# Two chained matrix products with a GELU between: an opening block that goes slice by slice, and fp32r operands in six of sixteen contraction tiles

## The chip, the cores and the metric

The kernel runs on one core of one Trainium2 chip. The core has several engines that run side by side and wait for each other through semaphores: PE (TensorE, matrix products; its weight loads are listed apart as PEld), DVE (VectorE), ACT (ScalarE), POOL (GpSimd) and SP (SyncE, which here only issues transfers). Sixteen DMA engines move data between HBM and the on-chip memory SBUF; PE writes its sums to a second on-chip memory, PSUM. The metric is the device time of one execution in microseconds (us); lower is better.

## The reference

```python
def setup_inputs():
    m, k, n, p = 1024, 1024, 2048, 1024      # a: m x k, b: k x n, c: n x p, all float32, normal
...
def reference(a, b, c):
    h = np.matmul(a, b)
    h = 0.5 * h * (1 + np.tanh(np.sqrt(2 / np.pi) * (h + 0.044715 * h ** 3)))
    return np.matmul(h, c).astype(np.float32)
```

The inputs are 4.19 MB (a), 8.39 MB (b) and 8.39 MB (c), the output is 4.19 MB. Each of the two products has 1024 x 1024 x 2048 multiplications. On PE that is 256 matmuls each, if one matmul takes a 128 x 128 stationary operand (the weights) and streams 512 columns past it.

## The kernel before, in words

All inputs are float32 in HBM; they are loaded into staging buffers, cast to bf16 and kept in SBUF. The rows of a are worked through in two chunks of 512 (mc = 0 and 1).

For each chunk `load_a_chunk` (L47) loads four row tiles of 128 x 1024, each by one transfer on the SP queue (L51), casts each on ACT (L53), and transposes it on PE in 32 pieces of 128 x 128 (L60, out to the PSUM tile `pt`), which DVE copies one by one into the eight tiles `aT` (L61). So `aT` is a chunk of a with the contraction index on the partitions.

Then comes the first product. Its result is made transposed, with n on the partitions: for each of 16 column tiles `nt` of b, eight matmuls over the contraction tiles `kt` are accumulated in one PSUM tile of 128 x 512 (L90); b is the stationary operand, `aT` is streamed. ACT applies the GELU on the way out of PSUM and writes the bf16 tile `hT` (L93). In chunk 0 b is loaded in four column slices of 512: `load_b_slice` (L65) issues eight transfers on SP (L68), and ACT casts each piece (L69). Before each column tile of chunk 0 `load_c` (L71) loads one 128 x 1024 tile of c on POOL's queue (L73), which DVE casts (L74). In chunk 1 b and c are there already.

The second product of the chunk follows (L96 to L105): for each of four row tiles and two halves of the columns, 16 matmuls over `nt` are accumulated (L100), with `hT` stationary and `c_sb` streamed; DVE copies the sum to SBUF (L104) and SP stores it (L105).

The order on each engine is settled by the tile framework's scheduler from the order of the program and from the dependences; the buffer counts of the pools (six staging buffers for a and b, three for c, three PSUM tiles for sums, two for transposes) decide how far a transfer or a product can run ahead. Transfers of one queue start in the order of their issue.

Of the kernel before, what the change touches and what calls it, by code (L numbers as in the profile page):

```python
# [1 line left out]

# [6 lines left out]

F32 = mybir.dt.float32  # L10
BF16 = mybir.dt.bfloat16
AF = mybir.ActivationFunctionType


@with_exitstack
def kernel(ctx, tc, a, b, c, out):
    nc = tc.nc
    M, K = a.shape
    _, N = b.shape
    _, P = c.shape  # L20
    KT = K // 128
    NT = N // 128
    MC = 512
    PC = 512
    BS = 512
    NSL = N // BS

    consts = ctx.enter_context(tc.tile_pool(name="consts", bufs=1))
    ident = consts.tile([128, 128], BF16)
    make_identity(nc, ident)  # L30

    bpool = ctx.enter_context(tc.tile_pool(name="bpool", bufs=KT))
    cpool = ctx.enter_context(tc.tile_pool(name="cpool", bufs=NT))
    stage = ctx.enter_context(tc.tile_pool(name="stage", bufs=6))
    cstage = ctx.enter_context(tc.tile_pool(name="cstage", bufs=3))

    abfpool = ctx.enter_context(tc.tile_pool(name="abfpool", bufs=5))
    atpool = ctx.enter_context(tc.tile_pool(name="atpool", bufs=KT + 2))
    hpool = ctx.enter_context(tc.tile_pool(name="hpool", bufs=NT + 2))
    psum = ctx.enter_context(tc.tile_pool(name="psum", bufs=3, space=bass.MemoryType.PSUM))  # L40
    psum_t = ctx.enter_context(tc.tile_pool(name="psum_t", bufs=2, space=bass.MemoryType.PSUM))
    opool = ctx.enter_context(tc.tile_pool(name="opool", bufs=4))

    b_sb = [bpool.tile([128, N], BF16, name="b_sb") for _ in range(KT)]
    c_sb = [cpool.tile([128, P], BF16, name="c_sb") for _ in range(NT)]

    def load_a_chunk(mc):  # L47
        a_bf = []
        for mt in range(MC // 128):
            st = stage.tile([128, K], F32, name="sta")  # L50
            nc.sync.dma_start(out=st, in_=a[ds(mc * MC + mt * 128, 128), :])  # L51
            t = abfpool.tile([128, K], BF16, name="a_bf")
            nc.scalar.activation(t, st, AF.Copy)  # L53
            a_bf.append(t)
        aT = []
        for kt in range(KT):
            at = atpool.tile([128, MC], BF16, name="aT")
            for mt in range(MC // 128):
                pt = psum_t.tile([128, 128], BF16, name="pt")
                nc.tensor.transpose(pt, a_bf[mt][:, ts(kt, 128)], ident)  # L60
                nc.vector.tensor_copy(at[:, ts(mt, 128)], pt)  # L61
            aT.append(at)
        return aT

    def load_b_slice(j):  # L65
        for kt in range(KT):
            st = stage.tile([128, BS], F32, name="stb")
            nc.sync.dma_start(out=st, in_=b[ts(kt, 128), ts(j, BS)])  # L68
            nc.scalar.activation(b_sb[kt][:, ts(j, BS)], st, AF.Copy)  # L69

    def load_c(nt):  # L71
        st = cstage.tile([128, P], F32, name="stc")
        nc.gpsimd.dma_start(out=st, in_=c[ts(nt, 128), :])  # L73
        nc.vector.tensor_copy(c_sb[nt], st)  # L74

    aT = load_a_chunk(0)
    hT_all = []
    for mc in range(M // MC):
        if mc > 0:
            aT = load_a_chunk(mc)  # L80
        hT = []
        for j in range(NSL):
            if mc == 0:
                load_b_slice(j)
            for nt in range(j * (NT // NSL), (j + 1) * (NT // NSL)):
                if mc == 0:
                    load_c(nt)
                ps = psum.tile([128, MC], F32, name="ps1")
                for kt in range(KT):
                    nc.tensor.matmul(ps, b_sb[kt][:, ts(nt, 128)], aT[kt],  # L90
                                     start=(kt == 0), stop=(kt == KT - 1))
                h = hpool.tile([128, MC], BF16, name="hT")
                nc.scalar.activation(h, ps, AF.Gelu_apprx_tanh)  # L93
                hT.append(h)

        for mt in range(MC // 128):  # L96
            for pc in range(P // PC):
                ps = psum.tile([128, PC], F32, name="ps2")
                for nt in range(NT):
                    nc.tensor.matmul(ps, hT[nt][:, ts(mt, 128)],  # L100
                                     c_sb[nt][:, ts(pc, PC)],
                                     start=(nt == 0), stop=(nt == NT - 1))
                ot = opool.tile([128, PC], F32, name="ot")
                nc.vector.tensor_copy(ot, ps)  # L104
                nc.sync.dma_start(out=out[ds(mc * MC + mt * 128, 128), ts(pc, PC)], in_=ot)  # L105


# [1 line left out]
_INS = ['a', 'b', 'c']  # L109
_OUTS = [((1024, 1024), 'float32')]  # L110


# [23 lines left out]
```

## Time and profile before

| what | value |
|---|---|
| time, median of the two runs shown | 195.03 us (157.47 and 232.58) |
| span of the profiled execution | 157.0 us (time of the run that it answers to: 157.47 us) |
| mean granted TensorE clock | 0.946 |
| PE busy | 125.8 us, 80% of the span |
| ACT, DVE, POOL busy | 47.6, 33.7, 9.3 us |
| read from HBM, written | 20.97 MB, 4.19 MB |
| transfers: time from issue to landing, median | a 7.9 us, b 7.5 us, c 6.8 us, output 2.0 us |

The profile is of one execution on the chip. A group line of the page reads: line of the kernel, engine, operation, what it writes and reads, shapes and types, how many, then busy time in us and mean ns of one, then the idle time of the engine just before these instructions and what ended it. In the strip of 40 slices each digit is the busy share of a slice of the span in tenths; PEclk is the granted clock of TensorE in tenths. Matmuls overlap in PE's pipeline, so the mean duration of one (from its start to its end) is longer than the distance between two starts. Some matmul records are missing from the trace, so the counts of matmuls are slightly below those of the code.

### The profile page before, as it was taken

How to read it: one execution, taken by the hardware profiler on the slowest of the kernel's cores; microseconds unless marked ns; L12 is line 12 of the kernel's file. 1: busy time of each engine (PE TensorE's matmuls, PEld its weight loads, DVE VectorE, ACT ScalarE, POOL GpSimd, SP SyncE). 2: the span in 40 equal slices, each digit the busy share in tenths (PEclk: the TensorE clock that was granted, in tenths of full speed). 3: DMA queues.
4: the chain of work that ended last, by engine and by line, in shares of the span. 5: the costliest groups of instructions: out<-in, count | busy, mean ns of one | idle time of the engine just before them, and what ended most of it. 6: DMA issues, size and time to landing. Idle time of an engine off the chain costs nothing.

```text
span 157.0 us, 1522 instructions
## 1 busy us (share of the span) xinstructions
PE 125.8 (80%) x565; PEld 56.4 (36%) x576; DVE 33.7 (21%) x96; ACT 47.6 (30%) x74; POOL 9.3 (6%) x22
## 2 busy tenths in 40 slices
PE   0104952729994699999999979999999999999990
PEld 0001421213441244444444434444444444444440
DVE  0022664423113100011122146600000002111111
ACT  3534734497563995300000000053343310000000
POOL 6010121221210000000000000000000000000000
PEclk9999997555999789999999999999999999999999
DMA  5999999999999930011111120000000001122111
GB/s 177 406 381 316 362 338 413 397 399 401 395 399 398 410 155 2 0 67 71 67 67 69 69 103 30 0 4 0 0 0 0 0 4 67 67 84 112 72 67 67
DMA packets 10375, 25.26 MB, mean 161 GB/s; under 512 B 1152, under 2 KB 1152, under 8 KB 10368
## 3 DMA queue, kind: packets, MB, share of 16 engines
q1 hardware_dynamic: 8064, 16.78, 29.0%
q0 software_dynamic: 2304, 8.39, 13.6%
q8 instruction: 4, 0.07, 0.2%
q14 instruction: 3, 0.02, 0.1%
HBM read 20.97 MB, written 4.19 MB: 160 GB/s over the span
## 4 chain that ended last, share of the span: by engine, by line
PE 62%; DMA 26%; ACT 5%; DVE 2%; SPq 2%; issue 1%
PE ps L100 35%; DMA stb<-in_b_dram 26%; PE ps L90 24%; ACT b_sb L69 3%; PE pt L60 2%; ACT hT L93 2%; SPq L51 1%; DVE aT L61 1%; DVE ot L104 1%; ACT L93 1%; SPq L68 1%
## 5 line engine op out<-in xcount | busy, mean ns | idle before, releaser
L90 PE MATMUL ps<-aT,b_sb 128*128 128x512 bf16 x250 | 66.8, 410 | 8.9 <-ACT hT L93 7.1
L100 PE MATMUL ps<-c_sb,hT 128*128 128x512 bf16 x251 | 55.3, 379 | 0.3
L90 PEld LDWEIGHTS <-b_sb 128*128 128x128 bf16 x256 | 26.2, 103 | 48.7 <-issue 20.3
L100 PEld LDWEIGHTS <-hT 128*128 128x128 bf16 x256 | 25.0, 98 | 30.2
L93 ACT ACTIVATE hT<-ps 128x512 bf16<-128x512 f32 x32 | 18.6, 594 | 56.7 <-PE ps L90 55.6
L104 DVE COPY ot<-ps 128x512 f32<-128x512 f32 x16 | 11.1, 692 | 81.8 <-PE ps L100 81.8
L60 PE MATMUL pt<-ident,a_bf 128*128 128x128 bf16 x64 | 13.3, 240 | 18.4 <-ACT a_bf L53 11.7
L69 ACT ACTIVATE b_sb<-stb 128x512 bf16<-128x512 f32 x32 | 19.8, 629 | 15.1 <-DMA stb<-in_b_dram 14.8
L74 DVE CAST c_sb<-stc 128x1024 bf16<-128x1024 f32 x16 | 11.1, 692 | 27.2 <-DMA stc<-in_c_dram 27.1
L61 DVE COPY aT<-pt 128x128 bf16<-128x128 bf16 x64 | 12.5, 220 | 11.4 <-PE pt L60 10.8
L60 PEld LDWEIGHTS <-a_bf 128*128 128x128 bf16 x64 | 6.7, 107 | 17.7 <-ACT a_bf L53 12.3
L73 POOL DMA_DIRECT2D stc<-in_c_dram x16 | 8.6, 539 | 35.1 <-DVE aT L61 23.0
L53 ACT ACTIVATE a_bf<-sta 128x1024 bf16<-128x1024 f32 x8 | 8.4, 1054 | 6.3 <-DMA sta<-in_a_dram 6.3
L53 ACT ACT_TABLE_LOAD x1 | 1.3, 1283 | 0.7 <-PEq L120 0.7
L93 ACT ACT_TABLE_LOAD x1 | 1.3, 1283 | 0.0
masks.py:199 POOL TENSOR_SCALAR_AFFINE_SELECT ident<-ident 128x128 bf16<-128x128 bf16 x1 | 0.3, 306 | 0.1
masks.py:197 POOL MEMSET ident<- 128x128 bf16 x1 | 0.2, 205 | 0.3 <-POOLq L120 0.3
L120 POOL MEMSET const-float32-0.0<- 128x1 f32 x1 | 0.1, 99 | 0.2 <-issue 0.2
L120 POOL MEMSET const-bfloat16-1.0<- 128x1 bf16 x1 | 0.1, 102 | 0.0
L120 POOL MEMSET const-uint8-127<- 128x1 uint8 x1 | 0.1, 102 | 0.0
L120 POOL MEMSET const-float32-1.0<- 128x1 f32 x1 | 0.1, 99 | 0.0
## 6 DMA issues: line engine op xcount, KB each, us to landing
stc<-in_c_dram POOLq DMA_DIRECT2D x16, 512.0 KB, 6.8
stb<-in_b_dram SPq DMA_DIRECT2D x32, 256.0 KB, 7.5
sta<-in_a_dram SPq DMA_DIRECT2D x8, 512.0 KB, 7.9
out_dram<-ot SPq DMA_DIRECT2D x16, 256.0 KB, 2.0
```

The lines of the kernel that those rows point to most:

```text
L51: nc.sync.dma_start(out=st, in_=a[ds(mc * MC + mt * 128, 128), :])
L53: nc.scalar.activation(t, st, AF.Copy)
L60: nc.tensor.transpose(pt, a_bf[mt][:, ts(kt, 128)], ident)
L61: nc.vector.tensor_copy(at[:, ts(mt, 128)], pt)
L68: nc.sync.dma_start(out=st, in_=b[ts(kt, 128), ts(j, BS)])
L69: nc.scalar.activation(b_sb[kt][:, ts(j, BS)], st, AF.Copy)
L73: nc.gpsimd.dma_start(out=st, in_=c[ts(nt, 128), :])
L74: nc.vector.tensor_copy(c_sb[nt], st)
L90: nc.tensor.matmul(ps, b_sb[kt][:, ts(nt, 128)], aT[kt], start=(kt == 0), stop=(kt == KT - 1))
L93: nc.scalar.activation(h, ps, AF.Gelu_apprx_tanh)
L100: nc.tensor.matmul(ps, hT[nt][:, ts(mt, 128)], c_sb[nt][:, ts(pc, PC)], start=(nt == 0), stop=(nt == NT - 1))
L104: nc.vector.tensor_copy(ot, ps)
```

## The change

The order on the engines is now that of the program, by a manual schedule. The kernel holds all of a transposed (`aT[k][h]`, two halves of 512 rows), b as one tile, and all of `hT`, and there is no longer a loop over row chunks.

- **Opening block.** a is loaded in eight slices along the contraction index (all 1024 rows x 128 columns, so rows of 512 bytes in HBM), each followed by the matching 128 rows of the first three column tiles of b. For each slice DVE casts two halves of a, ACT casts b, PE makes eight transposes into two PSUM tiles of 128 x 512, and DVE copies one of them and ACT the other into `aT`. The six sums of the first three column tiles (three tiles x two halves of rows) lie open in six PSUM tiles at once, and each slice adds six matmuls to them. The second half of a slice is done after the transposes of the next one. Ahead of it stand seven matmuls on zeros (they add to nothing that is kept) and one GELU of a single column.
- **Loads.** All loads go on the SP queue, but for the first piece of b, which ACT issues; DVE casts the rest of b and c, in transfers of 0.5 to 1 MB. POOL issues none.
- **First product, rest.** For each of the other 13 column tiles, two groups of eight matmuls, each followed by its GELU.
- **Second product.** 16 contraction tiles as before, for eight row tiles. The first six of them (R = 6) have `hT` and c in fp32r, a four-byte format that PE takes as an operand, written by ACT and DVE; the other ten stay bf16. For the last row tile the second half of the columns is made and stored in two parts of 256.

```diff
-    consts = ctx.enter_context(tc.tile_pool(name="consts", bufs=1))
...
+    ctx.enter_context(tc.manual_schedule())
+    astage = ctx.enter_context(tc.tile_pool(name="astage", bufs=4))
+    abf = ctx.enter_context(tc.tile_pool(name="abf", bufs=3))
+    b0stage = ctx.enter_context(tc.tile_pool(name="b0stage", bufs=4))
+    stage = ctx.enter_context(tc.tile_pool(name="stage", bufs=4))
+    ppool = ctx.enter_context(tc.tile_pool(name="ppool", bufs=6, space=PSUM))
+    tpool = ctx.enter_context(tc.tile_pool(name="tpool", bufs=2, space=PSUM))
...
+    R = 6
+    F32R = mybir.dt.float32r
+    c_r = keep.tile([128, R, P], F32R, name="c_r")
+    c_h = keep.tile([128, NT - R, P], BF16, name="c_h")
+    hT = [[keep.tile([128, H], F32R if t < R else BF16, name=f"hT{t}_{h}") for h in range(2)] for t in range(NT)]
...
+    for k in range(KT):
+        st = astage.tile([128, MT, 128], F32, name="a_st")
+        bt = b0stage.tile([128, W0], F32, name="b0_st")
+        if k == 0:
+            nc.sync.dma_start(out=st[:, 0:4, :], in_=av[:, 0:4, ts(k, 128)])
+            nc.scalar.dma_start(out=bt, in_=bv[:, k, 0:W0])
+            nc.sync.dma_start(out=st[:, 4:8, :], in_=av[:, 4:8, ts(k, 128)])
+        else:
+            nc.sync.dma_start(out=st, in_=av[:, :, ts(k, 128)])
+            nc.sync.dma_start(out=bt, in_=bv[:, k, 0:W0])
...
+    nc.scalar.activation(g, warm[:, 0:1], AF.Gelu_apprx_tanh)
+    for _ in range(7):
+        nc.tensor.matmul(wps, warm[:, 0:128], warm, start=True, stop=True)
...
+    def mm0(k, h):
+        for t in range(N0):
+            nc.tensor.matmul(ps[t][h], b_sb[:, k, ts(t, 128)], aT[k][h],
+                             start=(k == 0), stop=(k == KT - 1))
+    for k in range(KT):
+        ab = abf.tile([128, MT, 128], BF16, name="ab")
+        nc.vector.tensor_copy(ab[:, 0:4, :], a_st[k][:, 0:4, :])
+        nc.vector.tensor_copy(ab[:, 4:8, :], a_st[k][:, 4:8, :])
+        nc.scalar.activation(b_sb[:, k, 0:W0], b_st[k], AF.Copy)
+        for h in range(2):
+            pt = tpool.tile([128, H], BF16, name="pt")
+            for j in range(4):
+                nc.tensor.transpose(pt[:, ts(j, 128)], ab[:, 4 * h + j, :], ident)
+            if h == 0:
+                nc.vector.tensor_copy(aT[k][h], pt)
+            else:
+                nc.scalar.activation(aT[k][h], pt, AF.Copy)
+        if k > 0:
+            mm0(k - 1, 1)
+        mm0(k, 0)
+    mm0(KT - 1, 1)
+    def load_b(t0, nt):
+        w = nt * 128
+        kn = 2048 // max(w, 256)
+        for kh in range(0, KT, kn):
+            st = stage.tile([128, 2048], F32, name="st")
+            sv = st[:, 0:kn * w].rearrange("p (k n) -> p k n", k=kn)
+            nc.sync.dma_start(out=sv, in_=bv[:, kh:kh + kn, ds(t0 * 128, w)])
+            nc.vector.tensor_copy(b_sb[:, kh:kh + kn, ds(t0 * 128, w)], sv)
+    def load_c(t0):
+        st = stage.tile([128, 2048], F32, name="st")
+        sv = st.rearrange("p (t q) -> p t q", t=2)
+        nc.sync.dma_start(out=sv, in_=cv[:, t0:t0 + 2, :])
+        nc.vector.tensor_copy(c_r[:, t0:t0 + 2, :] if t0 < R else c_h[:, t0 - R:t0 - R + 2, :], sv)
...
+    def mm1(t):
+        for h in range(2):
+            p = ppool.tile([128, H], F32, name="ps")
+            for k in range(KT):
+                nc.tensor.matmul(p, b_sb[:, k, ts(t, 128)], aT[k][h],
+                                 start=(k == 0), stop=(k == KT - 1))
+            nc.scalar.activation(hT[t][h], p, AF.Gelu_apprx_tanh)
...
+    for mt in range(MT):
+        h, j = divmod(mt, 4)
+        for q0, w in ((0, 512), (512, 512)) if mt < MT - 1 else ((0, 512), (512, 256), (768, 256)):
+            p = ppool.tile([128, w], F32, name="ps", padded_shape=[128, H])
+            for t in range(NT):
+                nc.tensor.matmul(p, hT[t][h][:, ts(j, 128)], c_r[:, t, ds(q0, w)] if t < R else c_h[:, t - R, ds(q0, w)],
+                                 start=(t == 0), stop=(t == NT - 1))
+            store(mt, q0, w, p)
```

More of the change, by code (lines that the diff above doesn't have):

```diff
@@ L12 @@
 AF = mybir.ActivationFunctionType
+PSUM = bass.MemoryType.PSUM
 @with_exitstack
@@ L22 @@
     NT = N // 128
[L23 to L26, printed above, removed]
-    consts = ctx.enter_context(tc.tile_pool(name="consts", bufs=1))
-    ident = consts.tile([128, 128], BF16)
-    make_identity(nc, ident)
[L32 to L105, printed above, removed]
@@ new lines @@
+    b0stage = ctx.enter_context(tc.tile_pool(name="b0stage", bufs=4))
+    stage = ctx.enter_context(tc.tile_pool(name="stage", bufs=4))
+    opool = ctx.enter_context(tc.tile_pool(name="opool", bufs=4))
+    ppool = ctx.enter_context(tc.tile_pool(name="ppool", bufs=6, space=PSUM))
+    tpool = ctx.enter_context(tc.tile_pool(name="tpool", bufs=2, space=PSUM))
+    warm = consts.tile([128, H], BF16, name="warm")
+    nc.vector.memset(warm, 0.0)
+    ident = consts.tile([128, 128], BF16, name="ident")
@@ new lines @@
+    make_identity(nc, ident)
+    aT = [[keep.tile([128, H], BF16, name=f"aT{k}_{h}") for h in range(2)] for k in range(KT)]
+    b_sb = keep.tile([128, KT, N], BF16, name="b_sb")
+    R = 6
[3 more added lines that the diff above has]
+    hT = [[keep.tile([128, H], F32R if t < R else BF16, name=f"hT{t}_{h}") for h in range(2)] for t in range(NT)]
+    a_st, b_st = [], []
+    for k in range(KT):
[8 more added lines that the diff above has]
+            nc.sync.dma_start(out=bt, in_=bv[:, k, 0:W0])
+        a_st.append(st)
+        b_st.append(bt)
@@ new lines @@
+    g = consts.tile([128, 1], F32, name="g")
+    nc.scalar.activation(g, warm[:, 0:1], AF.Gelu_apprx_tanh)
+    wps = tpool.tile([128, H], F32, name="pt")
+    for _ in range(7):
+        nc.tensor.matmul(wps, warm[:, 0:128], warm, start=True, stop=True)
+    ps = [[ppool.tile([128, H], F32, name="ps") for _ in range(2)] for _ in range(N0)]
+    def mm0(k, h):
+        for t in range(N0):
+            nc.tensor.matmul(ps[t][h], b_sb[:, k, ts(t, 128)], aT[k][h],
+                             start=(k == 0), stop=(k == KT - 1))
@@ new lines @@
+    load_b(3, 1)
+    load_b(4, 1)
+    for h in range(2):
+        for t in range(N0):
+            nc.scalar.activation(hT[t][h], ps[t][h], AF.Gelu_apprx_tanh)
+    def mm1(t):
+        for h in range(2):
+            p = ppool.tile([128, H], F32, name="ps")
[3 more added lines that the diff above has]
+            nc.scalar.activation(hT[t][h], p, AF.Gelu_apprx_tanh)
@@ new lines, with store @@
+    load_b(5, 1)
+    load_b(6, 2)
+    load_b(8, 4)
+    load_b(12, 4)
+    for t in range(0, NT, 2):
+        load_c(t)
+    for t in range(N0, NT):
+        mm1(t)
+    def store(mt, q0, w, p):
+        ot = opool.tile([128, w], F32, name="ot", padded_shape=[128, H])
+        nc.vector.tensor_copy(ot, p)
+        nc.sync.dma_start(out=out[ts(mt, 128), ds(q0, w)], in_=ot)
+    for mt in range(MT):
[6 more added lines that the diff above has]
+            store(mt, q0, w, p)
```

8 lines of the change are left out of this document (added).

## Prediction

> **What bounds the kernel now.** I began with the page's engine shares, its strip of 40 slices (3.9 us each) and the chain of waits, to see which stage is limited by what.
>
> ```profile
> span 157.0 us, 1522 instructions
> PE 125.8 (80%) x565; PEld 56.4 (36%) x576; DVE 33.7 (21%) x96; ACT 47.6 (30%) x74; POOL 9.3 (6%) x22
> ...
> PE   0104952729994699999999979999999999999990
> ...
> PEclk9999997555999789999999999999999999999999
> DMA  5999999999999930011111120000000001122111
> GB/s 177 406 381 316 362 338 413 397 399 401 395 399 398 410 155 2 0 67 71 67 67 69 69 103 30 0 4 0 0 0 0 0 4 67 67 84 112 72 67 67
> ...
> HBM read 20.97 MB, written 4.19 MB: 160 GB/s over the span
> ...
> PE ps L100 35%; DMA stb<-in_b_dram 26%; PE ps L90 24%; ACT b_sb L69 3%; PE pt L60 2%; ACT hT L93 2%; SPq L51 1%; DVE aT L61 1%; DVE ot L104 1%; ACT L93 1%; SPq L68 1%
> ```
>
> There are two regimes. For the first 14 slices the DMA engines are full and PE is in pieces; from slice 14 DMA is nearly idle and PE is solid. All 20.97 MB are read in the first regime. The chain agrees: 26% of it is waiting for b, the rest mostly matmuls. The next rows, of the table by stretch, give rates and clock; the columns are the stretch, its length, busy time (and instructions) of PE, PEld, DVE, ACT, POOL, then granted clock, DMA share, GB/s. The last is for the second matmul alone (PE, PEld).
>
> ```profile
> 2.00:2.50 0.50, 0.00 (x0) 0.00 (x0) 0.00 (x0) 0.02 (x1) 0.47 (x2) 1.00 0.48 156
> 2.50:3.00 0.50, 0.00 (x0) 0.00 (x0) 0.00 (x0) 0.00 (x0) 0.50 (x2) 1.00 0.91 369
> 5.00:12.00 7.00, 0.86 (x3) 0.31 (x3) 1.18 (x4) 2.88 (x4) 0.53 (x1) 1.00 1.00 383
> 12.00:24.00 12.00, 7.40 (x39) 3.70 (x40) 6.29 (x26) 6.40 (x11) 1.59 (x3) 1.00 0.99 346
> 24.00:36.00 12.00, 5.73 (x20) 2.29 (x21) 4.12 (x13) 7.85 (x13) 2.64 (x5) 0.56 1.04 403
> ...
> 137.23:148.02 10.79, 10.74 (x49) 4.90 (x50) 1.00 0.19 73
> ```
>
> The last row holds 50 weight loads (one matmul record is missing), so a 512-column bf16 matmul costs 10.79 / 50 = 0.216 us when they follow one another. The code has 256 such matmuls in each product: 55.3 us each, 110.6 us together. So 157.0 us is this floor plus some 46 us in which loads and PE fail to overlap. The change aims at that part, and puts a new price on some of the matmuls.
>
> **The change part by part.** The durations come from the page's groups and the chain.
>
> ```profile
> L100 PE MATMUL ps<-c_sb,hT 128*128 128x512 bf16 x251 | 55.3, 379 | 0.3
> ...
> L100 PEld LDWEIGHTS <-hT 128*128 128x128 bf16 x256 | 25.0, 98 | 30.2
> L93 ACT ACTIVATE hT<-ps 128x512 bf16<-128x512 f32 x32 | 18.6, 594 | 56.7 <-PE ps L90 55.6
> L104 DVE COPY ot<-ps 128x512 f32<-128x512 f32 x16 | 11.1, 692 | 81.8 <-PE ps L100 81.8
> ...
> L69 ACT ACTIVATE b_sb<-stb 128x512 bf16<-128x512 f32 x32 | 19.8, 629 | 15.1 <-DMA stb<-in_b_dram 14.8
> L74 DVE CAST c_sb<-stc 128x1024 bf16<-128x1024 f32 x16 | 11.1, 692 | 27.2 <-DMA stc<-in_c_dram 27.1
> L61 DVE COPY aT<-pt 128x128 bf16<-128x128 bf16 x64 | 12.5, 220 | 11.4 <-PE pt L60 10.8
> ...
> L53 ACT ACT_TABLE_LOAD x1 | 1.3, 1283 | 0.7 <-PEq L120 0.7
> ```
>
> ```profile
> 96.83 0.22 PE L60 MATMUL pt<-ident,a_bf 128*128 128x128 bf16 x1
> 97.85 0.27 PE L60 MATMUL pt<-ident,a_bf 128*128 128x128 bf16 x2
> ```
>
> ```profile
> 125.74 0.65 PE ps L100 x3
> ...
> 153.40 0.69 DVE ot L104
> ```
>
> *Opening, DMA.* All of a and three column tiles of b are queued first: 4.19 + 1.57 = 5.77 MB. Data flow at the full rate from about 2.3 us (the 2.00 and 2.50 rows; the first issue keeps its place). At 390 GB/s, between the rows with 383 and 403, they are there at 2.3 + 14.8 = 17.1 us. But a now comes in runs of 512 B, where the trace has runs of 4 KB (a, c) and 2 KB (b). Nothing here shows 512 B. Its ends: no cost, or half the rate, 4.19 / 0.390 = 10.7 us more. A gain is excluded, since the engines' share is already 1.0. The known runs differ by a factor of two with no visible loss, so I stay near the low end: +1.5 us, 18.6 us.
>
> *Opening, engines, for one slice of a* (18.6 - 2.3 = 16.3 over 8 slices: 2.04 us). PE: 8 transposes, the second of a pair adding 0.055 us (0.27 against 0.22), and 6 matmuls: 0.44 + 1.30 = 1.74. DVE: two casts of 512 columns, each between half of 692 ns and 692, taken at 0.43, and one copy of 512 out of PSUM, between 0.22 and 0.69, taken at 0.43: 1.3 us, at worst 2.07. ACT: a cast of 384 columns, under the 629 ns of 512, and a copy of about 594: 1.2. So DMA paces the opening and the engines hide behind it. That cover is thin for PE (0.3 us), and DVE at its worst would come level. If the clock fell to the 0.56 of the 24 to 36 row, PE would need 1.74 / 0.56 = 3.1 us per slice, 8.5 us more in all; but the rows at 12 to 24 kept 1.00 with PE 62% busy, and here it would be 85%.
>
> *End of the opening.* After the last slice lands: two casts 0.86, four transposes 0.22 + 3 x 0.055 = 0.39, the nine matmuls still queued 1.94, handoffs 0.1: 3.3 us, so 21.9. Six PSUM buffers are full then; the first GELU (0.59) can start when the first of them closes, five matmuls or 1.1 us earlier, so the next group finds a free one. A group of eight takes 1.73 us and its GELU 0.59: ACT stays hidden.
>
> *First product, the other 13 column tiles:* 13 x 2 x 8 = 208 matmuls, 44.9 us: 66.8. What could be late is b. Tiles 3 to 5 follow in the same queue, 0.52 MB each, about 1.5 us apart, while PE uses one per 3.5 us. c comes last: 18.6 + 1.57 MB at 350 + 13.63 MB at 400 (4.5 + 34.1) = 57.2 us, 9.6 us before it is needed; those 9.6 us are the cover.
>
> *Moved waits.* All loads but one now sit on SP in one order, and each waits for a staging buffer that DVE casts free; behind a waiting load stand all later ones, and the stores. The stores start after 70 us, when the loads are done. On DVE the casts stand ahead of the output copies; also done by then. One MB takes 2.6 us to arrive and, at the 692 ns per 512 columns of the slowest row, at most 2.8 to cast, and 1.4 if the 692 per 1024 of L74 holds, so DVE costs nothing, or 0.2 per MB off the path. POOL's 16 issues vanish; they were beside the path. The table load (1.28) and seven warming matmuls fall before the first data.
>
> *Second product, if bf16:* 240 full matmuls and 32 of half width, 55.3 us by columns: 122.1. *Tail:* from the chain, 157.0 - 153.40 = 3.6 us after the last matmul; a copy of 256 columns for one of 512 saves 0.27: 3.3, span 125.4. The profiled execution took 157.47 us for a span of 157.0: 125.9.
>
> *fp32r.* 6 of 16 contraction tiles in 17 groups: 90 full and 12 half matmuls, 102 with 96 full ones' worth of columns. No 4-byte operand of PE is in this trace. A gain is excluded: the columns are as many, and the clock is already 1.00. The upper end is four passes, 3 x 0.216 x 96 = 62.2 us. I take one pass at the bf16 pace, because the row nearest to it is the same shape at 0.216, and its weight load (98 ns) lies under the preceding matmul, with room for one of twice the bytes (196 ns). What is left is 34 changes of type, each between 0 and one unpipelined matmul, 379 - 216 = 163 ns, 5.5 us in all; I take a fifth, 1.1. Wider ACT and DVE writes of the 4-byte tiles: 0, under the covers above.
>
> Sum: 2.3 + 16.3 + 3.3 + 44.9 + 55.3 + 3.3 + 0.5 + 1.1 = **127.0 us**. It stands against 157.5 of the profiled execution. The median of 195.03 is of two runs, 157.47 and 232.58; nothing in the trace explains the second, and I forecast an execution like the first. Own range of this case: 124 (no loss from 512 B, no changes of type) to 133.
>
> **The rivals.**
>
> *The 4-byte weight load isn't hidden.* If PE cannot load the next weights while a matmul streams, each of 102 pays 98 ns, 10.0 us: 136; with the refill of the pipeline as well, 98 + 163 ns, 26.6 us: 152.5. For it: no 4-byte load is shown. Against it: in the bf16 rows the loads hide completely. Middle 144. The Trainium skill, "TensorE: Matmul & The Clock Gate", section "Weight-path perf modes — Fast Weight Load (FWL) and DoubleRow", says that reading weights 32 bits at a time gives 32-bit weights no win and that the fast load is only on for types other than FP32. That speaks against the change; no run here shows it. A load of twice the length would be 196 ns; hidden, it exceeds its cover only in the 12 half matmuls (196 - 108 ns, 1.1 us: 127); exposed and with the refill, 102 x 0.359 = 36.6 us: 162.5, slower than before.
>
> *Half rate.* Twice the bytes per column at the same bytes per time: 96 x 0.216 = 20.7: 147.
>
> *Four passes: slower.* If the 4-byte matmul runs as four products of split operands, the second product takes 55.3 + 62.2 us: 188. It decides against the change as soon as each pays over 31.6 / 96 = 0.33 us more, 2.5 times the bf16 cost. Nothing in the trace speaks for or against. The Trainium skill, "FP8 and Floating Point Precision", section "TensorE Precision Notes", gives four passes for true FP32 and sets beside it a reduced-precision form that reads four bytes and truncates; I take fp32r for the second, and no run here shows it.
>
> *Short runs at half rate.* 10.7 in place of 1.5 in the opening: 136, with the first GELU about 31 us in. Against it: the equal rates of 2 and 4 KB.
>
> **How the numbers follow.** Chances: forecast 0.52; load exposed 0.20, doubled and exposed 0.03; half rate 0.08; four passes 0.08; short runs 0.09. The range of 123 to 150 holds the forecast, the short runs, most of the exposed load and of the half rate: 0.82. Within 2% (154.3 to 160.6, about what can be told from no change) lies hardly a case: 0.02. Faster: the forecast, short runs, half rate, exposed load, less their edges: 0.88. Slower: 0.10.
>
> **What would show it.** In the changed kernel: stretches of the second product with 16 matmuls per 3.45 us, and an fp32r group whose busy mean is near 379 ns; 500 ns or more would mean the second or third rival. The first GELU of a real tile at about 21 us; at 30 it is the short runs or the clock, told apart by the granted clock and the GB/s of the first 20 us. PE idle between 22 and 122 us under 2 us; a wait of L-lines of the first product on b, or of the second on c, would break the 9.6 us of cover. The forecast is wrong if the second product takes over 62 us or the opening over 27.

## The result, and the profile after

The changed kernel takes 133.02 us (two runs, 132.23 and 133.81) and is faster: the ratio to the kernel before is 0.844, 95% interval 0.834 to 0.854. Run again later it was 0.850 (0.845 to 0.855). The 232.58 us that make the median of before 195.03 us did not come back in 21 later executions of that kernel (156.66 to 159.92 us), and the ratio leaves them out.

The page of the changed kernel, the lines that answer to those of before (the strip has slices of 3.3 us here):

```profile
span 132.0 us, 1458 instructions
...
PE 123.3 (93%) x599; PEld 64.0 (48%) x599; DVE 38.9 (29%) x58; ACT 29.0 (22%) x50; POOL 0.7 (1%) x6
...
PE   6499998789999999999999999999999999999990
...
PEclk9999999999999999999999999999999999999999
DMA  3999999999999999997000022222221112222231
GB/s 39 286 308 311 306 310 308 295 316 367 393 386 403 405 408 414 407 410 284 7 0 5 0 79 79 79 79 79 79 79 61 55 53 76 79 79 79 79 122 40
...
PE ps L152 43%; PE ps L129 34%; DMA st<-in_b_dram 6%; PE ps L82 5%; DMA a_st<-in_a_dram 4%; PE pt L93 2%; SPq L68 1%; DVE b_sb L111 1%; ACT aT L97 0%; DVE ab L88 0%; SPq L63 0%; DVE ot L144 0%
```

The two regimes of before have merged. PE is solid from the third slice on, with a dip in the seventh to ninth, while DMA is full for the first 18 slices: the loads of c now run beside the first product. The chain was 26% b-load before; it is now 84% PE. What stands out against it is the first 28 us, where the DMA engines are full but move 286 to 316 GB/s, not the 367 to 414 of later. The granted clock rose too: the row of before falls to 5 to 8 tenths in slices 7 to 10, 14 and 15, the row above has 9 (90% or more) throughout. What part of the gain is the clock's was not tested apart; the 21 later executions of the kernel before had mean clocks of 0.941 to 0.978, and their times differ by 3.3 us in all, against a gain of some 24 us.

The chain of waits in order of time gives the bounds of the stages (start, length, what):

```profile
18.25 7.77 DMA st<-in_b_dram
...
26.04 0.71 DVE b_sb L111
...
26.79 45.07 PE ps L129 x208
71.86 56.85 PE ps L152 x272
...
128.73 0.42 DVE ot L144
```

And the timeline of the opening, with the idle time before each piece in brackets:

```profile
5.60 0.43 DVE L87 CAST ab<-a_st 128x512 bf16<-128x512 f32 x1 [4.47 <-DMA a_st<-in_a_dram]
...
6.51 0.43 DVE L88 CAST ab<-a_st 128x512 bf16<-128x512 f32 x1 [0.48 <-DMA a_st<-in_a_dram]
...
8.29 0.43 DVE L87 CAST ab<-a_st 128x512 bf16<-128x512 f32 x1 [1.02 <-DMA a_st<-in_a_dram]
...
9.61 2.77 PE L82 MATMUL ps<-aT,b_sb 128*128 128x512 bf16 x6
...
12.71 1.46 PE L82 MATMUL ps<-aT,b_sb 128*128 128x512 bf16 x6
...
22.37 0.43 DVE L87 CAST ab<-a_st 128x512 bf16<-128x512 f32 x1 [0.99 <-DMA a_st<-in_a_dram]
...
22.84 0.52 ACT L89 ACTIVATE b_sb<-b_st 128x384 bf16<-128x384 f32 x1 [0.96 <-DMA b_st<-in_b_dram]
...
23.42 2.10 PE L82 MATMUL ps<-aT,b_sb 128*128 128x512 bf16 x9
...
26.04 0.69 DVE L111 CAST b_sb<-st 128x1024 bf16<-128x1024 f32 x1 [2.33 <-DMA st<-in_b_dram]
```

The first half of the first slice of a is cast at 5.60 us and its second half at 6.51; the second slice follows at 8.29 and the eighth at 22.37, so a slice takes (22.37 - 8.29) / 6 = 2.35 us. DVE waits about 1 us for each slice in the later part: transfers set the pace. SP waited as well before its loads of b (4.5 us for ACT, in four pieces), but the DMA engines stayed full meanwhile: their mean share from 4.5 to 26 us is 1.17. The opening ends at 23.42 + 2.10 = 25.52 us, but the fourth column tile of b is cast only from 26.04, so PE stands still until 26.79. From there on it does not stop again: 45.07 us for the rest of the first product, 56.85 for the second.

The groups of the second product, by form (busy us, mean ns of one):

```profile
L152 PE MATMUL ps<-c_h,hT 128*128 128x512 bf16 x150 | 35.0, 380 | 0.0
L152 PE MATMUL ps<-c_r,hT 128*128 128x512 f32 x90 | 25.8, 422 | 0.0
...
L152 PEld LDWEIGHTS ps<-c_r,hT 128*128 128x128 f32 x102 | 18.6, 189 | 4.8
L152 PEld LDWEIGHTS <-hT 128*128 128x128 bf16 x170 | 15.3, 98 | 18.3 <-issue 3.9
```

An fp32r weight load takes 189 ns, nearly twice the 98 of bf16, and an fp32r matmul 422 in place of 380 from start to end. The second product as a whole is only 1.55 us longer than 55.3, the forecast for bf16.

### The profile page after: what moved, and what is told of

The parts are those of the page before. It is cut to its first block, busy times and chain, and to the rows that moved or that the text cites. A ratio compares the mean times of both kernels' runs of the same rounds, so it can differ in the third digit from the quotient of the medians.

```text
span 132.0 us, 1458 instructions
## 1 busy us (share of the span) xinstructions
PE 123.3 (93%) x599; PEld 64.0 (48%) x599; DVE 38.9 (29%) x58; ACT 29.0 (22%) x50; POOL 0.7 (1%) x6
## 3 DMA queue, kind: packets, MB, share of 16 engines
HBM read 20.97 MB, written 4.19 MB: 191 GB/s over the span
## 4 chain that ended last, share of the span: by engine, by line
PE 84%; DMA 10%; DVE 1%; SPq 1%; ACT 0%; issue 0%
PE ps L152 43%; PE ps L129 34%; DMA st<-in_b_dram 6%; PE ps L82 5%; DMA a_st<-in_a_dram 4%; PE pt L93 2%; SPq L68 1%; DVE b_sb L111 1%; ACT aT L97 0%; DVE ab L88 0%; SPq L63 0%; DVE ot L144 0%
## 5 line engine op out<-in xcount | busy, mean ns | idle before, releaser
L129 PE MATMUL ps<-aT,b_sb 128*128 128x512 bf16 x208 | 45.1, 379 | 1.3 <-DVE b_sb L111 1.3
L152 PE MATMUL ps<-c_h,hT 128*128 128x512 bf16 (+1 forms) x170 | 37.5, 368 | 0.0
L152 PE MATMUL ps<-c_r,hT 128*128 128x512 f32 (+1 forms) x102 | 27.9, 408 | 0.0
L144 DVE COPY ot<-ps 128x512 f32<-128x512 f32 (+1 forms) x17 | 11.2, 660 | 53.0 <-PE ps L152 53.0
L152 PEld LDWEIGHTS <-hT 128*128 128x128 bf16 x170 | 15.3, 98 | 18.3 <-issue 3.9
L131 ACT ACTIVATE hT<-ps 128x512 bf16<-128x512 f32 (+1 forms) x26 | 15.5, 597 | 29.4 <-PE ps L129 29.4
L152 PEld LDWEIGHTS ps<-c_r,hT 128*128 128x128 f32 x102 | 18.6, 189 | 4.8
L82 PE MATMUL ps<-aT,b_sb 128*128 128x512 bf16 x48 | 13.6, 427 | 0.0
L111 DVE CAST b_sb<-st 128x2048 bf16<-128x2048 f32 (+1 forms) x8 | 8.2, 1027 | 12.6 <-DMA st<-in_b_dram 12.6
L93 PE MATMUL pt<-ident,ab 128*128 128x128 bf16 x64 | 6.5, 245 | 3.0 <-DVE ab L87 2.7
L87 DVE CAST ab<-a_st 128x512 bf16<-128x512 f32 x8 | 3.4, 427 | 9.7 <-DMA a_st<-in_a_dram 9.7
L88 DVE CAST ab<-a_st 128x512 bf16<-128x512 f32 x8 | 3.4, 421 | 0.5 <-DMA a_st<-in_a_dram 0.5
```

The lines of the kernel that those rows point to most:

```text
L82: nc.tensor.matmul(ps[t][h], b_sb[:, k, ts(t, 128)], aT[k][h], start=(k == 0), stop=(k == KT - 1))
L87: nc.vector.tensor_copy(ab[:, 0:4, :], a_st[k][:, 0:4, :])
L88: nc.vector.tensor_copy(ab[:, 4:8, :], a_st[k][:, 4:8, :])
L93: nc.tensor.transpose(pt[:, ts(j, 128)], ab[:, 4 * h + j, :], ident)
L111: nc.vector.tensor_copy(b_sb[:, kh:kh + kn, ds(t0 * 128, w)], sv)
L129: nc.tensor.matmul(p, b_sb[:, k, ts(t, 128)], aT[k][h], start=(k == 0), stop=(k == KT - 1))
```

## The experiments

### Transfers alone: run length or queue

The loads of the opening, without any product, in stretches that differ in one thing. Short form of the edit:

```diff
+    for i in range(8):    # a, runs of 512 B; then 1 KB, 4 KB; b in 512 B, 2 KB
+        t = tile("a512")
+        nc.sync.dma_start(out=t.rearrange("p (m k) -> p m k", m=8), in_=av[:, :, ts(i, 128)])
+        use(t)
...
+        (nc.scalar if i % 2 else nc.sync).dma_start(...)    # last: 512 B runs from SP and ACT in turn
```

> Transfers alone: no matmul, no cast; 512 KB transfers into a ring of eight buffers, in stretches that differ in run length and queue: a in runs of 512 B, 1 KB, 4 KB, b in runs of 512 B and 2 KB, all on SP, then a and b in runs of 512 B issued by SP and ACT in turn. It leaves out both products and writes rows of c to the output. My theory: 512 B runs give 280 to 320 GB/s on either queue arrangement, 1 KB about 360, 2 and 4 KB about 400. Rival, one queue as the limit: the stretches with two queues reach 400 with 512 B runs. Rival, neither: all stretches give 400 and the opening was slow because of casts and buffer slots.

The table by stretch of this kernel; the columns are the stretch, its length, DVE and POOL busy time, clock, DMA share, GB/s. In order: a in 512 B runs, a in 1 KB, a in 4 KB, b in 512 B, b in 2 KB, both in 512 B from two queues.

```profile
6.00:14.00 8.00, 0.86 (x5) 0.00 (x0) 1.00 1.20 291
22.00:28.00 6.00, 0.67 (x5) 0.00 (x0) 1.00 1.10 348
32.00:38.00 6.00, 0.85 (x5) 0.00 (x0) 1.00 1.02 408
44.00:62.00 18.00, 1.72 (x10) 0.00 (x0) 1.00 1.20 290
74.00:86.00 12.00, 1.55 (x9) 0.00 (x0) 1.00 1.05 387
98.00:126.00 28.00, 2.20 (x16) 0.00 (x0) 1.00 1.20 290
```

In these stretches the rate follows the run length alone: 290, 348, 387, 408 GB/s for 512 B, 1, 2 and 4 KB. Which input it is makes no difference, and a second queue none either (290). Per DMA engine these rates are 28, 47, 85 and 160 ns per run (16 x run length / rate), which a fixed 9.4 ns per run and 37.7 ns per KB reproduce; both numbers are fitted, not seen. Applied to the opening: 512 KB of a at 290 is 1.81 us, 192 KB of b in runs of 1,536 B by the fit 0.53 us, together 2.34 us per slice or 308 GB/s. The changed kernel shows just that: 2.35 us per slice, and 308 GB/s from 5.57 to 22.37 us. The theory holds; the queue and the buffer slots fall as causes of the slow opening.

### Longer runs in the kernel: the gain that turned into a wait

```diff
-            nc.sync.dma_start(out=st, in_=av[:, :, ts(k, 128)])
+            st = astage.tile([128, 4, 256], F32, name="a_st")    # 4 row tiles x 256 columns
+            nc.sync.dma_start(out=st, in_=av[:, ds(4 * i, 4), ds(k2 * 128, 256)])
```

> The changed kernel with a loaded in pieces of 4 row tiles x 256 columns, so in runs of 1 KB in place of 512 B; bytes, number of transfers, queue, casts and matmuls are the same. My theory is that the opening is paced by the transfers of a in runs of 512 B (about 305 GB/s from 6 to 25 us, where 2 and 4 KB runs reach 404): then the rate in that stretch rises to 350 GB/s or more, a slice takes 2.0 us in place of 2.34, and the first matmul of the first product's rest moves from 26.8 to about 24 us, the span to about 129.5. Rival: the single SP queue, or the slots of the staging buffers, set the pace; then rate and span stay within 0.5 us.

Ratio 0.848 (0.841 to 0.854), spans 131.6 to 132.3 us: no gain. The issues of SP (start, length) show why:

```profile
4.60 1.56 SPq L68 DMA_DIRECT2D b_st<-in_b_dram  x1
9.32 0.37 SPq L62 DMA_DIRECT2D a_st<-in_a_dram  x1
...
10.81 0.45 SPq L68 DMA_DIRECT2D b_st<-in_b_dram  x1
15.23 0.37 SPq L62 DMA_DIRECT2D a_st<-in_a_dram  x1
```

And what SP waited for up to 30 us (in all, times, longest):

```profile
SPq L62 <- DVE ab L87: 7.2, 2, 4.2
```

A staging buffer now holds two slices' columns and comes free only when the second has been cast. With four buffers SP issued nothing for 3 to 4 us, twice, and the queue ran dry: the strip of this kernel falls from 362 and 349 GB/s to 250 and 214. The rest of the first product, which I expected at about 24 us, started at 26.80. The rate rose where nothing waited; the time went to the wait. The casts that free the buffers were themselves held up by PE here: until 14 us its matmuls of 512 columns stood 0.427 us apart, and the chain of waits runs through PE from 8.68 to 14.81.

So the next version took eight buffers each for a and the first tiles of b. The room for them came from R = 0, all bf16: with fp32r kept there was not room in SBUF for even six buffers of a (the output buffers need 8 KB per partition, 2.56 KB were left), so more buffers alone, at R = 6, have no result.

```diff
-    astage = ctx.enter_context(tc.tile_pool(name="astage", bufs=4))
+    astage = ctx.enter_context(tc.tile_pool(name="astage", bufs=8))
-    b0stage = ctx.enter_context(tc.tile_pool(name="b0stage", bufs=4))
+    b0stage = ctx.enter_context(tc.tile_pool(name="b0stage", bufs=8))
-    R = 6
+    R = 0
```

> Three edits at once: a in runs of 1 KB (4 row tiles x 256 columns), eight staging buffers each for a and for the first tiles of b, so that no load of the opening waits for a buffer, and R = 0, which makes the room for them. Theory: the opening is paced by the run length (512 KB in 1.81 us at 512 B, 1.51 us at 1 KB in the kernel of transfers alone), and the first attempt with 1 KB lost this to waits for buffers (no transfer of a issued from 4.6 to 9.3 us and from 11.3 to 15.2 us). Then the first matmul of the rest of the first product moves from 26.7 to 22 to 23 us, the second product takes 55.3 us, and the span is about 126 to 127 us. Rival: the opening is bound by PE and the chain from slice to slice; then that matmul stays at 26 us or later and the span at 130.5.

Ratio 0.829 (0.824 to 0.834), 130.69 us: better than both kernels, but short of the forecast, and part of it is R = 0 (all bf16 alone gives 0.835, below). Lines of its timeline:

```profile
7.32 0.43 DVE L86 CAST ab<-a_st 128x512 bf16<-128x512 f32 x1 [6.19 <-DMA a_st<-in_a_dram]
...
21.01 0.43 DVE L87 CAST ab<-a_st 128x512 bf16<-128x512 f32 x1 [0.87 <-DMA a_st<-in_a_dram]
...
25.41 1.89 PE L128 MATMUL ps<-aT,b_sb 128*128 128x512 bf16 x8
```

The larger first piece lands later (cast at 7.32, not 5.60), PE starts later and, as the next experiments show, at half pace, and has no slack to make it up at 1.74 us per slice. The last piece of a (half the rows of the last two slices) is there at 21.01, 1.4 us earlier than the last slice of the changed kernel, and the first product's rest starts at 25.41, also 1.4 earlier. PE waits only 0.41 us for that piece and then has 4.1 us of work left in the opening. The rival was half right: PE had become the next bound, close behind the transfers.

### The slow start of PE

In the changed kernel's timeline above six matmuls take 2.77 us at 9.61 and 1.46 at 12.71, that is 0.427 and 0.215 us apart, while every entry of the granted-clock row says 1.00. The trace resolves this: it holds no clock record before 12.35 us, and the row prints 1.00 where there is none. In the kernel with groups of 256 columns (below), whose records begin earlier, matmuls stand 0.215 us apart at 7.4 us, where the clock is 1.00, and 0.427 apart from 9.66 on, where it is 0.50. More warming matmuls in place of seven:

```diff
-    for _ in range(7):
+    for _ in range(16):
```

> The changed kernel with 16 warming matmuls in place of 7. In the changed kernel matmuls of 512 columns follow each other at 0.427 us until 12 us and at 0.215 after, though the row of granted clock says 1.00. If the opening is paced by the transfers, a faster start of PE moves nothing after 15 us: first matmul of the rest of the first product at 26.5 to 26.8, span 131.5 to 132.3. If the slow start is on the path, it comes 1.5 to 2 us earlier.

Chain and timeline of this kernel:

```profile
26.61 6.00 PE ps L129 x27
```

```profile
9.24 1.46 PE L82 MATMUL ps<-aT,b_sb 128*128 128x512 bf16 x6
```

With sixteen the first real matmuls run at full pace (1.46 us at 9.24), and the opening still ends where it did: 26.61 against 26.79 (and 26.54 when the changed kernel ran again), spans 131.7 to 132.1, ratio 0.851 (0.844 to 0.858). The slow start is real and hidden behind the transfers, as the first branch expected.

The last version joins this with short pieces (512 B runs) for the first two and last two slices, and 1 KB runs for the four between:

```diff
+    for k in (0, 1, 2, 4, 6, 7):
+        n = 2 if k in (2, 4) else 1
+        for i in range(2):
+            st = astage.tile([128, 4, 128 * n], F32, name="a_st", padded_shape=[128, 4, 256])
+            nc.sync.dma_start(out=st, in_=av[:, ds(4 * i, 4), ds(k * 128, 128 * n)])
```

> All bf16 (R = 0), eight staging buffers each, 16 warming matmuls, a in halves of 512 B runs for the first two and last two slices (short first and last steps) and 1 KB runs for the four between. Worked out from the kernel of transfers alone: slices at 2.34 us, pairs at 4.07: last slice at about 20.5 us, rest of the first product from 23.9 us, span 127.5 us; against 130.2 for R = 0 alone and 129 for the first attempt with 1 KB runs. Rival: PE, 1.74 us per slice and cold at the start, holds it at 25 us: span 129.

Ratio 0.829 (0.814 to 0.844), spans of 127.9 to 129.6 us: no better than the version before it, and all above the 127.5 expected. PE now finishes the opening at 24.52, and then waits for the fourth column tile of b, as this line of its timeline shows:

```profile
24.97 0.69 DVE L114 CAST b_sb<-st 128x1024 bf16<-128x1024 f32 x1 [2.17 <-DMA st<-in_b_dram]
```

What bounds the opening moved from the slices to this tile. Its run length is not the whole reason: it comes 3.29 us after the last piece of a (cast at 21.68), where 0.52 MB in 512 B runs took 1.81 us with transfers alone. The part on the prediction comes back to this.

### What fp32r costs

All bf16, nothing else changed (R = 0, the last two lines of the diff two sections up):

> The changed kernel with R = 0: all sixteen contraction tiles of the second product in bf16, nothing else different. My theory is that fp32r runs in one pass and costs only about 0.09 us where a group of six fp32r matmuls meets the bf16 ones (the second product takes 56.85 us from first matmul to last copy, against 55.3 us for 256 bf16 matmuls at 0.216). Then the second product shrinks by 1.3 to 1.6 us, the span goes from 132.0 to about 130.5 us, and the first matmul of the first product's rest stays at 26.8 us. Rival: fp32r has no price at all and the 1.5 us are something else in this loop; then the span stays at 132.0. Rival: the four-byte c and hT also delay the loads or the GELUs; then the opening or the first product shortens too.

Ratio 0.835 (0.827 to 0.844). The second product took 55.30 us, 1.55 less than with fp32r, and the opening still ended at 26.61. So the price is real, and it sits in the second product: the rest of the first took 45.07 us in both. Two other traces with bf16 alone have 55.31 too. Four with the same fp32r part have 56.85 (the changed kernel and its repetition), 57.13 (sixteen warming matmuls) and 57.14 (1 KB runs), so the price is 1.55 to 1.84 us. The spans (128.9 to 130.5, against 131.8 to 132.3 of the changed kernel run again) say the same, though one of its first two executions had 130.4.

The fp32r part alone in the old kernel:

```diff
-    c_sb = [cpool.tile([128, P], BF16, name="c_sb") for _ in range(NT)]
+    c_sb = [(crpool.tile([128, P], F32R, name="c_r") if t < R else cpool.tile([128, P], BF16, name="c_sb")) for t in range(NT)]
...
-                h = hpool.tile([128, MC], BF16, name="hT")
+                h = hrpool.tile([128, MC], F32R, name="hTr") if nt < R else hpool.tile([128, MC], BF16, name="hT")
```

> The kernel before, with only the fp32r part of the change: tiles 0 to 5 of hT and c are fp32r, everything else as it was. A price of about 0.1 us per group of sixteen matmuls (14 ns per fp32r matmul and 14 ns where the type changes, as read from the starts of the matmuls) times 16 groups adds 1.6 us: span 1.6 us longer than that of the kernel before, ratio 1.01. If the four-byte operands cost more where loads and matmuls run side by side, over 1.02.

Ratio 1.016 (1.009 to 1.022). Its chain of waits, the second chunk's second product:

```profile
125.55 1.39 PE ps L104 x6
...
154.11 0.69 DVE ot L108
```

28.56 us where the kernel before had 27.66 (125.74 to 153.40): 0.11 us per group of sixteen, as expected. So the two parts of the change add up (0.835 x 1.016 = 0.848, measured 0.844 and 0.850): fp32r takes back 1.2 to 1.6%, and all else together gives the gain. No run undoes the opening, the order of the loads or the loss of the chunk loop alone, so their shares are open.

Where in a group the price arises was tried by mixing the types:

```diff
-            for t in range(NT):
+            for i, t in enumerate((0, 6, 1, 7, 2, 8, 3, 9, 4, 10, 5, 11, 12, 13, 14, 15)):
```

> The changed kernel with the sixteen contraction tiles taken in the order 0, 6, 1, 7, 2, 8, 3, 9, 4, 10, 5, 11, 12 to 15, so that fp32r and bf16 alternate: six stretches of fp32r per group of sixteen where there was one; the number of fp32r matmuls is the same. If the price sits at the change of type (about 0.09 us per stretch in the changed kernel), 17 groups x 5 more stretches x 0.09 = 7.7 us are added: span near 139.5 us. If the price is one per fp32r matmul (1.5 us over 102 of them), the span stays at 132.0 us. If a longer weight load hides only under a preceding matmul of 512 columns, nothing changes either, since all but the last two groups have that.

The second product alone, by stretch (PE, PEld, clock, DMA share, GB/s), in the mixed kernel:

```profile
71.90:130.13 58.23, 58.22 (x267) 27.43 (x271) 1.00 0.19 71
```

and in the changed kernel:

```profile
71.86:128.71 56.85, 56.84 (x272) 33.51 (x271) 1.00 0.19 72
```

Six stretches per group add 1.38 us, neither 7.7 nor nothing: both theories fall in their pure form. With two unknowns the two runs solve: 17 x (6p + c) = 1.55 and 17 x (6p + 6c) = 2.93 give p = 12.5 ns for each fp32r matmul and c = 16 ns for each stretch of them. Two numbers from two runs prove nothing by themselves. The starts in the traces agree: in the changed kernel fp32r matmuls of 512 columns mostly start 226 to 233 ns apart, bf16 ones 216, and the first two bf16 starts behind a stretch are late as well (230 and 227); in the mixed kernel a pair of fp32r and bf16 takes 460 ns in place of 432. With sixteen warming matmuls the fp32r starts are 235 ns apart, so the price per matmul is known to some 3 ns only. A third case was to bear the values out: groups half as wide, in which a weight load has half the cover.

```diff
-        for q0, w in ((0, 512), (512, 512)) if mt < MT - 1 else ((0, 512), (512, 256), (768, 256)):
+        for q0, w in ((0, 256), (256, 256), (512, 256), (768, 256)):
```

> The changed kernel with every group of the second product 256 columns wide (32 groups of sixteen half-width matmuls), six tiles fp32r. If the price of fp32r is a weight load that takes about 140 ns per load when loads follow one another (189 ns of one, 47 ns of it overlapped), it no longer hides under a half-width matmul of 108 ns: about 33 ns per fp32r matmul, 0.20 us per group as in the last two groups of the changed kernel (1.93 us in place of 1.73), so the second product takes 55.3 + 32 x 0.20 = 61.7 us. If the price is the same per matmul as at full width (14 ns each and 14 ns at the change), 32 x 0.098 = 3.1 us: 58.4 us.

> As the kernel with groups of 256 columns, but all sixteen tiles bf16: the second product takes 55.3 to 55.9 us if bf16 loads hide under half-width matmuls (98 ns for one, under 55 ns apart when they follow one another). If it takes much longer, the narrow width alone has a price and the fp32r price must be taken against this run.

The chains of the two kernels, fp32r first:

```profile
70.50 58.25 PE ps L152 x512
```

```profile
70.44 55.91 PE ps L152 x512
```

The difference is 2.34 us over 32 groups, 73 ns per group. The theory of a weight load that sticks out of a half-width matmul wanted 200; a price per matmul and stretch wanted 6 x 12.5 + 16 = 91 by the solved values. So the longer load does not hold up the matmuls even at half width (190 ns for one load, while fp32r matmuls start 118 to 120 ns apart and bf16 ones 109), and the price is of the second kind, though somewhat lower here. What it is inside PE stays open.

Last, what the slower rival would have been: true float32 in the same six tiles.

```diff
-    F32R = mybir.dt.float32r
+    F32R = F32
```

> The changed kernel with true float32 in place of fp32r for the six tiles of hT and c; bytes, casts and order are the same. If float32 takes four passes where fp32r takes one, the second product takes 55.3 + 62.2 = 117.5 us or somewhat more, and the span is 193 us or more: what the slower rival of the prediction would have been. If fp32r and float32 run alike, 56.9 and 132.

The time is 194.1 us (one execution), against 157.3 of the kernel before beside it. Its chain, and its groups:

```profile
71.96 117.00 PE ps L152 x374
```

```profile
L152 PE MATMUL ps<-c_r,hT 128*128 128x512 f32 x180 | 79.7, 592 | 0.0
...
L152 PEld LDWEIGHTS ps<-c_r,hT 128*128 128x128 f32 x204 | 38.7, 190 | 38.7 <-issue 35.9
```

(117.0 - 55.3) / 96 = 0.643 us more per full matmul, three times 0.214: the time of four passes. The trace shows two matmuls for each one of the program (180 records for 90), 429 ns apart where bf16 has 216, each with a weight load of its own (204 for 102). So four bytes as such are nearly free; the split into passes is not.

The changed kernel run again beside some of these:

> The changed kernel itself, beside the next ones on the same chip. Span 130.4 to 132.0 us as in its first two runs; 1.8 us of each execution lie outside the span.

Spans of 131.8 to 132.3 us, and again 1.8 us outside the span.

## Why the prediction was right or wrong

The direction, the mechanism of the opening and the choice among the rivals were right: faster by far, fp32r as one pass at the bf16 pace. The forecast was 127.0 us and a ratio of 127.0 / 157.5 = 0.806. Measured were 133.8 us in the profiled run and 0.844: the gain was overstated by a quarter. The first GELU of a real tile came at 24.48 us, where the forecast had named 21. The 6.8 us sit in these terms:

| term | forecast | measured | off by |
|---|---|---|---|
| last slice of a ready for its cast | 18.6 | 22.37 | +3.8 |
| chain to the end of the opening | 3.3 | 3.15 | -0.15 |
| wait for the fourth tile of b | 0 | 1.27 | +1.27 |
| rest of the first product | 44.9 | 45.07 | +0.17 |
| second product with fp32r | 56.4 | 56.85 | +0.45 |
| tail to the end of the span | 3.3 | 3.29 | 0 |
| outside the span | 0.47 | 1.81 | +1.34 |

**The step that failed is the price of short runs.** The prediction put it at +1.5 us, near the low end of its bounds, on the ground that runs of 2 and 4 KB show no visible difference. Transfers alone show that this was the wrong reading: 387 and 408 GB/s are the flat end of a curve with a fixed cost per run, and at 512 B it gives 290. For a this is 4.19 / 0.290 - 4.19 / 0.390 = 3.7 us, 2.2 more than the term held. The rival of short runs named the right mechanism and gave it 0.09, with half the rate, 10.7 us, as its only size; the truth lay a third of the way. The trace of before could not have told it: its rows at full DMA share range from 346 to 403 GB/s, wider than the step from 4 to 2 KB (408 to 387).

**The start was mis-sized too.** With data at the full rate from 2.3 us the first slice would be there at 2.3 + 2.04 = 4.34; its second half was cast at 6.51. That is 2.2 of the 3.8 us of the first row. The other 1.6 are the slices after it: 15.86 us from 6.51 to 22.37 against 7 x 2.04 = 14.3, and less than the 2.2 above, mainly because the forecast also counted the last piece of b. Run length does not explain the start: with transfers alone, 512 B runs as well, the rate was 247 GB/s at 2.0 to 2.5 us and 342 in the next half, while the changed kernel had 68 to 97 from 2.0 to 3.5 and 330 only from 4.0. Its first transfers stand on two queues, SP's and ACT's; no run tests whether that is why, so the cause stays open.

**The cover that broke** is b, which the forecast had a wait of 0 for. "About 1.5 us apart" for tiles 3 to 5 (the fourth to sixth) used 350 GB/s; these are 512 B runs as well, 1.81 us with transfers alone. But that does not make the wait. The last slice of b is there at 22.84, so the fourth tile would be cast at 24.65 and PE, busy until 25.52, would not wait. It was cast at 26.04, 3.2 us behind; the next two came 1.74 and 1.72 us later. In the kernel with groups of 256 columns, whose opening is the same, it went as the run length has it:

```profile
22.93 0.52 ACT L89 ACTIVATE b_sb<-b_st 128x384 bf16<-128x384 f32 x1 [0.96 <-DMA b_st<-in_b_dram]
...
24.67 0.69 DVE L111 CAST b_sb<-st 128x1024 bf16<-128x1024 f32 x1 [0.89 <-DMA st<-in_b_dram]
...
25.44 4.91 PE L129 MATMUL ps<-aT,b_sb 128*128 128x512 bf16 x22
```

There the fifth tile was late, at 27.24, and PE had no wait. What both have is one transfer of instructions: a packet of 16,384 bytes that holds one DMA engine for 1.21 us from 23.48 in the changed kernel and for 1.15 us from 23.20 in this one. All eleven traces with this opening, or with its versions above, have such a packet between 22.6 and 24.5 us, and in each a tile of b due soon after comes 0.5 to 1.5 us late. That the packet is the cause is likely, but not shown.

The cover for c held: the last cast of c ends at 64.9 us, 7 us before the second product, not 9.6.

**The clock.** The prediction argued that it would stay up and named 8.5 us as the price if not. In the profiled run PE ran at half pace until 12.2 us, by the distance of the matmuls, but the transfers covered it; with sixteen warming matmuls the time did not change. Right in the sum, for the wrong reason.

**fp32r.** Taken at 1.1 us, measured 1.55 in the profiled run and up to 1.84 in others. It was put at the changes of type only; the runs give some 12 ns or more on every fp32r matmul as well. That the guess of a fifth came near was luck. The page of the Trainium skill that spoke against the change ("TensorE: Matmul & The Clock Gate", section "Weight-path perf modes — Fast Weight Load (FWL) and DoubleRow") has the direction right: the load takes 189 ns, not 98, close to the 196 estimated from twice the bytes. But it hides, and the estimate of 162.5 us built on an exposed load is refuted. The four passes that the Trainium skill gives in "FP8 and Floating Point Precision", section "TensorE Precision Notes", are confirmed for float32 by the experiment with true float32 (117.0 us); fp32r, at 56.85 us, runs as one pass.

**Outside the span.** I paired the span of 157.0 us with the time of 157.47. In nearly all later runs, of either kernel, time and span differ by 1.7 to 2.0 us (in three by 2.5 to 3.0), so that pairing was probably wrong, and 1.3 us of the miss come from this term. Which of the two listed times belongs to the profiled span cannot be told from what was recorded.

## What to carry to other kernels

Price a load by its run length, not by its bytes alone: a change of layout that makes slices available earlier can cost more in rate than it gains in order, and the opening of a kernel is where nothing hides it. When a stage is made faster, look at once for what is late next and for what the faster pieces hold on to: here, in turn, buffer slots, PE's own 1.74 us per slice, and the one tile that PE needs after the opening. And to say what an operand type costs, undo that part alone: fp32r looked heavy by its rows (422 ns, loads twice as long) and cost 1.6 to 1.8 us of 132.

## What the runs showed of the hardware that was not expected

- 290, 348, 387 and 408 GB/s at runs of 512 B, 1, 2 and 4 KB, and 290 at 512 B with two queues as with one; a fixed cost of some 9 ns per run and DMA engine fits this.
- The row of granted clock said 1.00 while matmuls of 512 columns stood 0.427 us apart, up to 12 us into the changed kernel, because the trace has no record there; the distance between matmuls is the safer reading.
- With the same seven warming matmuls and 1.5 to 1.8 us of nothing behind them the slow stretch differed between executions: until 12.2 us in the profiled one, until 9.3 when it ran again, and from 8.3 to 11.7 with groups of 256 columns. Sixteen warming matmuls, up to the first data, gave full pace from 6 us on in both traces that have them.
- fp32r beside bf16: about 12 ns more per matmul and 16 ns per stretch, by two traces, and some 3 ns more per matmul in two others; true float32 in the same place 643 ns more per matmul of 512 columns.
